# Four pairs instead of three by seven products in part two's down projection, with its left sides summed earlier

## The chip, the cores and the metric

The kernel runs on one core of a Trainium2 chip. The metric is the device time of one execution in microseconds (us); the number shown for a kernel is the median of several executions. Engines are named as in the profile: PE is TensorE's matmul, PEld its weight load, DVE VectorE, ACT ScalarE, POOL GpSimd, SP SyncE.

## The reference

One decoder layer on 256 tokens of width 2048, all in float32. Only its feed-forward halves matter here; there are two of them (before and after the token mixer), alike in shape:

```python
def swiglu(x, w_gu, w_down):
    gate, up = jnp.split(x @ w_gu, 2, axis=-1)
    return (jax.nn.silu(gate) * up) @ w_down

h = h + 0.5 * swiglu(rms_norm(h, ffn1_norm[i]), ffn1_w_gu[i], ffn1_w_down[i])
h = h + hybrid_mixer(...)
h = h + 0.5 * swiglu(rms_norm(h, ffn2_norm[i]), ffn2_w_gu[i], ffn2_w_down[i])
h = h + sigmoid(rms_norm(h, ple_norm[i]) @ ple_w_gate[i]) * (p[i] @ ple_w_proj[i])
```

`w_gu` is 2048 x 11264, `w_down` 5632 x 2048. Gate and up are each 11 blocks of 512 columns; the down projection sums over 5632 = 22 pairs of 256 rows.

## The kernel before

**Float32 by three matmuls.** Each matrix is split into a high part (rounded to the fp32r format) and a low part (the rest). A product is high x high + high x low + low x high: three matmuls of 128 x 128 by 128 x 512. For a weight, ACT makes the high part (`whi`, `shi`, a cast), DVE the low part (`wlo`, `slo`, a subtraction).

**Plain pairs.** A pair is 256 rows of a weight block of 512 columns, 512 KB. SP loads it into one of four buffers `raw`; ACT and DVE split it; PE does 2 row blocks x 2 token halves x 3 = 12 matmuls with it.

**Seven products.** Two weight blocks of 512 columns belong together, and a pair of rows over both of them is a 2 x 2 product of 2 x 2 blocks: 8 block products, 24 matmuls. For the first `ns` pairs of a group the kernel uses a scheme with seven products instead of eight (Winograd's form of Strassen's). Product i multiplies one right side (a quarter of the weights, or a sum of quarters) with one left side (a quarter of the activations, or a sum), and one call of `product` does it for all `ns` pairs: 3 x `ns` matmuls. The right sides come from four quarters that are loaded whole, each 128 x (512 `ns`) floats: B11 is `raw[0, 0]`, B12 `raw[0, 1]`, A12's partner `raw[1, 0]`, and `raw[1, 1]`. `all_sums` makes them one after the other: it casts and subtracts (`shi`, `slo`) and then adds the next quarter into `raw[0, 0]`. Such an addition is done by DVE (`add`, tile R) or by a DMA from POOL's queue which reads the quarter again from HBM and adds it in flight (`add_loaded`, line 314). `SEVEN` is the order of the seven.

**Left sides.** `halves` makes the sums of activations: per pair, DVE adds high and low part to S (128 x 512, line 456), does four additions on quarters of it (128 x 128, line 462), ACT casts it to `Sh`, DVE subtracts to `Sl`. `Sh` and `Sl` have one buffer each, which gate/up and down share in turn.

**Staging.** The 11 blocks are worked in three parts of 3, 4 and 4 (`PARTS`; part two is blocks 3 to 6). For each block in turn PE computes gate and up (a "gu" group), and DVE and ACT make `silu(gate) * up`, which is transposed through a scratch tensor in DRAM (`tb`, `scr2`, `tT`) and split into `hTh`, `hTl`. After the part's blocks come two "dn" groups, one for output columns 0 to 1023 (`nb` = 0) and one for 1024 to 2047, whose products are added to `h`. The seven products of a group are interleaved with the plain pairs of the group before it, one product after each plain pair: products of part two's first dn group lie among the plain pairs of the part's last gu group.

**What sets the order.** `plan` writes lists of plain pairs, products and loads; `order` says in which order weights are asked for. `lanes` are generators that are stepped once per plain pair, so that side work is spread out. Below that, a scheduler places the instructions on each engine; `tc.keep_in_program_order` pins an instruction. Each engine then runs its queue strictly in order.

**Buffers that matter.** `shi` and `slo` have two buffers each: the cast for product n + 2 waits until PE has finished product n. `raw` quarters (tile R) have four homes; a group's quarters are loaded into homes that the group before it has finished with.

**Part sizes before.** `NS_DOWN` is 2, 3 and 3 pairs by seven for the three parts; a gu group has `NS` = 4.

## Time and profile before

| | |
|---|---|
| time, median of 3 runs | 1944.34 us (1944.25 to 1946.11) |
| the profiled execution, its own time | 1945.28 us |
| its span, first to last instruction | 1943.6 us |
| PE busy | 1928.1 us, 99% of the span |
| DVE busy | 1570.4 us, 81% |
| ACT busy | 1164.1 us, 60% |
| DMA read and written | 475.05 MB, mean 244 GB/s |
| granted TensorE clock | 0.999 |

How to read it: times are microseconds from the start of the span. A matmul's row has a duration of some 0.39 us, but matmuls overlap; what counts is the distance from one start to the next. "idle before, releaser" is how long the engine stood still before the instruction and what ended that. Part two's down begins among gate and up of block 6, at 346 us in the first feed-forward and at 1489 us in the second; part three's at 593 and 1736 us.

### The profile page before, as it was taken

What the parts mean: (1) busy time and instruction counts of PE and PEld (TensorE: products, weight loads), DVE (VectorE), ACT (ScalarE), POOL (GpSimd) and SP (SyncE); (2) the same over time, 40 slices, a digit from 0 to 9 for tenths busy, and PEclk for the clock granted to TensorE, in tenths of its full rate; (3) what the DMA queues carried; (4) which work ended last, traced back from release to release, by engine and by line L of the source; (5) the groups of instructions that cost most, each with busy time, mean ns of one, the idle gap of its engine ahead of it and who ended that gap; (6) DMA issues with size and microseconds to landing.
All of it is one profiled execution on the core that took longest, in us unless ns stands there. A gap on an engine that the chain in (4) does not pass through costs nothing.

```text
span 1943.6 us, 24163 instructions
## 1 busy us (share of the span) xinstructions
PE 1928.1 (99%) x8884; PEld 1594.0 (82%) x8884; DVE 1570.4 (81%) x1703; ACT 1164.1 (60%) x1362; POOL 148.4 (8%) x226
## 2 busy tenths in 40 slices
PE   9999999999999999999999999999999999999998
PEld 7888888888888888878788888888888888888886
DVE  7879878997789766797856579899888987888865
ACT  6656666666666557664555456566556755657654
POOL 0010110000010000010100000010000100001000
PEclk9999999999999999999999999999999999999999
DMA  8778898888888765556565776788888987989764
GB/s 307 269 236 282 252 293 285 237 288 249 280 285 242 228 218 171 176 169 211 161 213 159 244 283 231 226 281 289 248 275 241 327 264 244 271 237 314 234 214 143
DMA packets 144182, 475.05 MB, mean 244 GB/s; under 512 B 19648, under 2 KB 47296, under 8 KB 129856
## 3 DMA queue, kind: packets, MB, share of 16 engines
q1 hardware_dynamic: 107200, 302.16, 44.4%
q0 software_dynamic: 25920, 160.44, 30.2%
q10 hardware_dynamic: 10944, 10.91, 1.8%
q8 instruction: 69, 1.13, 0.2%
q14 instruction: 49, 0.40, 0.1%
HBM read 451.44 MB, written 22.02 MB: 244 GB/s over the span
## 4 chain that ended last, share of the span: by engine, by line
PE 92%; DVE 5%; DMA 2%; issue 1%; ACT 0%; POOL 0%; SPq 0%; POOLq 0%; DVEq 0%; ACTq 0%
PE d L550 5%; PE d L552 5%; PE d L551 5%; PE u L551 5%; PE u L552 5%; PE u L550 5%; PE g L343 5%; PE g L342 5%; PE g L344 5%; PE g L551 4%; PE g L552 4%; PE pj L112 4%; PE pj L113 4%; PE pj L114 4%; PE g L550 4%; PE d L344 3%
## 5 line engine op out<-in xcount | busy, mean ns | idle before, releaser
L77 ACT CAST whi<-raw 128x1024 fp32r<-128x1024 f32 (+1 forms) x489 | 511.3, 1049 | 401.1 <-PE pj L114 106.6
L78 DVE TENSOR_TENSOR wlo<-raw,whi 128x1024 fp32r<-128x1024 f32 (+1 forms) x489 | 592.0, 1218 | 162.9 <-ACT whi L77 161.8
L299 DVE TENSOR_TENSOR slo<-R,shi 128x2048 fp32r<-128x2048 f32 (+2 forms) x224 | 444.9, 1989 | 132.1 <-ACT shi L298 130.1
L298 ACT CAST shi<-R 128x2048 fp32r<-128x2048 f32 (+2 forms) x224 | 373.9, 1671 | 141.5 <-DVE R L307 62.7
L112 PE MATMUL pj<-whi,nTh 128*128 128x512 f32 x448 | 179.4, 401 | 0.0
L113 PE MATMUL pj<-wlo,nTh 128*128 128x512 f32 x448 | 175.2, 391 | 1.1 <-DVE wlo L78 1.1
L114 PE MATMUL pj<-whi,nTl 128*128 128x512 f32 x448 | 174.9, 390 | 0.0
L550 PE MATMUL d<-whi,hTh 128*128 128x512 f32 x448 | 174.5, 390 | 0.0
L551 PE MATMUL d<-wlo,hTh 128*128 128x512 f32 x448 | 174.4, 389 | 0.0
L552 PE MATMUL d<-whi,hTl 128*128 128x512 f32 x448 | 173.4, 389 | 0.0
L551 PE MATMUL g<-wlo,nTh 128*128 128x512 f32 x400 | 156.6, 391 | 0.6 <-DVE wlo L78 0.6
L552 PE MATMUL g<-whi,nTl 128*128 128x512 f32 x400 | 156.0, 390 | 0.0
L551 PE MATMUL u<-wlo,nTh 128*128 128x512 f32 x400 | 155.8, 389 | 0.2 <-DVE wlo L78 0.2
L552 PE MATMUL u<-whi,nTl 128*128 128x512 f32 x400 | 155.6, 389 | 0.0
L550 PE MATMUL g<-whi,nTh 128*128 128x512 f32 x400 | 155.0, 391 | 0.6 <-ACT nTh L161 0.6
L550 PE MATMUL u<-whi,nTh 128*128 128x512 f32 x400 | 153.4, 389 | 0.0
L307 DVE TENSOR_TENSOR R<-R 128x2048 f32<-128x2048 f32 (+2 forms) x68 | 135.7, 1996 | 0.1
L113 PEld LDWEIGHTS pj<-wlo,nTh 128*128 128x128 f32 x448 | 84.2, 188 | 18.9 <-DVE wlo L78 2.7
L550 PEld LDWEIGHTS d<-whi,hTh 128*128 128x128 f32 x448 | 84.1, 188 | 18.1 <-ACT hTh L504 1.0
L552 PEld LDWEIGHTS d<-whi,hTl 128*128 128x128 f32 x448 | 84.1, 188 | 17.8
L114 PEld LDWEIGHTS pj<-whi,nTl 128*128 128x128 f32 x448 | 84.1, 188 | 17.6
L551 PEld LDWEIGHTS d<-wlo,hTh 128*128 128x128 f32 x448 | 84.1, 188 | 17.4
(332 smaller groups left out, 3447.0 us busy)
## 6 DMA issues: line engine op xcount, KB each, us to landing
raw<-in_w_gu SPq DMA_DIRECT2D x199, 512.0 KB, 5.8
raw<-in_w_down SPq DMA_DIRECT2D x112, 512.0 KB, 6.4
raw<-in_w_in SPq DMA_DIRECT2D x112, 512.0 KB, 3.4
R<-in_w_gu2q POOLq DMA_DIRECT2D x54, 1024.0 KB, 8.6
R<-in_w_gu1q POOLq DMA_DIRECT2D x48, 1024.0 KB, 8.3
raw<-in_w_out SPq DMA_DIRECT2D x32, 512.0 KB, 4.3
tT<-scr SPq DMA_DIRECT2D x22, 512.0 KB, 5.8
R<-in_w_down11q POOLq DMA_DIRECT2D x12, 768.0 KB, 7.0
```

The source lines that it names most:

```text
L77: nc.scalar.copy(hi[:, j, :], raw[:, j, :])
L78: nc.vector.tensor_tensor(out=lo[:, j, :], in0=raw[:, j, :], in1=hi[:, j, :], op=ALU.subtract)
L112: nc.tensor.matmul(outs[t], xh[:, c], whi[:, j, :], start=st, stop=False)
L113: nc.tensor.matmul(outs[t], xh[:, c], wlo[:, j, :], start=False, stop=False)
L114: nc.tensor.matmul(outs[t], xl[:, c], whi[:, j, :], start=False, stop=sp)
L298: keep(nc.scalar.copy(hi, w))
L299: nc.vector.tensor_tensor(out=lo, in0=w, in1=hi, op=ALU.subtract)
L307: keep(nc.vector.tensor_tensor(out=self.raw[x], in0=self.raw[x], in1=self.raw[y], op=ALU.add))
L344: nc.tensor.matmul(out, xl, whi[:, g, :], start=False, stop=sp, skip_group_check=True)
L550: nc.tensor.matmul(out, xh[:, c], whi[:, j, :], start=st, stop=False, skip_group_check=True)
L551: nc.tensor.matmul(out, xh[:, c], wlo[:, j, :], start=False, stop=False, skip_group_check=True)
L552: nc.tensor.matmul(out, xl[:, c], whi[:, j, :], start=False, stop=sp, skip_group_check=True)
```

## The change

- Part two's dn groups treat four pairs by seven products instead of three: quarters of 1 MB instead of 768 KB, products of 12 matmuls instead of 9, and four plain pairs per block of 512 columns instead of five.
- In the first dn group of parts two and three the order of the seven is `SEVEN_DOWN`: the product with A12, whose quarter `raw[1, 0]` needs no sum, comes second, and that quarter is loaded second.
- In the same groups B11 + B12 is no longer added by DVE but by a DMA from POOL's queue that reads B12 again.
- The first two left sides of these groups are summed one gu group earlier (`first_sides`), and only split where they were summed before; the others are summed straight from the transposed block `tT` rather than from `hTh` + `hTl`. Their additions on the way are no longer all where they were pinned.
- The part's last block is given one step less of distance in part two (`last`).

```diff
--- before.py
+++ after.py
@@ -28,10 +28,11 @@
 NS = 4
-NS_DOWN = tuple(3 if i1 - i0 == 4 else 2 for i0, i1 in PARTS)
+NS_DOWN = (2, 2), (4, 4), (3, 3)
...
 SEVEN = (0, 1, 2, 4, 3, 5, 6)
+SEVEN_DOWN = (0, 4, 1, 2, 3, 5, 6)
@@ -257,6 +258,7 @@
...
+            self.seven = SEVEN_DOWN if kind == "dn" and part and nb == 0 else SEVEN
@@ -283,7 +285,7 @@
...
-            use = (0, 0), (0, 1), (1, 1), (1, 0)
+            use = ((0, 0), (0, 1), (1, 1), (1, 0)) if self.seven is SEVEN else ((0, 0), (1, 0), (0, 1), (1, 1))
             self.home = dict(zip(use, free))
             return [("load", lambda q=q: self.load(*q)) for q in use]
@@ -313,10 +315,10 @@
...
-            for i in SEVEN:
+            for i in self.seven:
                 ws = halved(*((0, 0), (0, 0), (0, 0), (0, 1), (1, 0), (1, 1), (0, 0))[i])
                 if i == 0:
-                    add((0, 0), (0, 1))
+                    (add if self.seven is SEVEN else add_loaded)((0, 0), (0, 1))
                     add_loaded((0, 1), (1, 1))
                 elif i == 1:
                     add((0, 0), (1, 1))
@@ -371,8 +373,9 @@
...
             for nb in (0, 2):
-                src = [sources(f"w_down{n}{p}", nb + b) for b in range(2)]
-                groups.append(Group("dn", p, [x[0] for x in src], [x[1] for x in src], NS_DOWN[p], len(groups) % 2, nb))
+                src = [sources(f"w_down{n}{p}{nb // 2}", b) for b in range(2)]
+                groups.append(Group("dn", p, [x[0] for x in src], [x[1] for x in src], NS_DOWN[p][nb // 2],
+                                    len(groups) % 2, nb))
@@ -420,11 +423,8 @@
...
-    def halves(kind, his, los, ns, wait=0, at_once=2):
-
-
-        for _ in range(wait):
-            yield
+    def left_sides(kind, his, los):
+
         fp = current[0]
@@ -439,38 +439,64 @@
...
         sides[kind] = side
-
-        for g0 in range(0, ns, at_once):
-            n = min(at_once, ns - g0)
-            k0 = 2 * (g0 % 2)
-            hi, lo = (x[g0 // 2][:, k0:k0 + 2 * n] for x in (his, los))
-            keep = lambda ins: ins
-            if g0 == 2 and n == 1:
-
-                keep = tc.keep_in_program_order
-                yield
-            if n == 2:
-                x = fp.tile([P, 2 * NB], F32, tag="sil", name="S")
-            else:
-                x = act.tile([P, NB], F32, tag="nat", name="S", bufs=4)
-            keep(nc.vector.tensor_tensor(out=x, in0=hi.bitcast(F32).rearrange("p k x -> p (k x)"),
-                                         in1=lo.bitcast(F32).rearrange("p k x -> p (k x)"), op=ALU.add))
-            xv = x.rearrange("p (g j t y) -> p g j t y", g=n, j=2, t=2)
-            a11, a12, a21, a22 = (xv[:, :, j, t, :] for t in range(2) for j in range(2))
-            for o, y, z, op in ((a22, a21, a22, ALU.subtract), (a21, a11, a21, ALU.subtract),
-                                (a11, a22, a11, ALU.subtract), (a12, a11, a12, ALU.add)):
-                nc.vector.tensor_tensor(out=o, in0=y, in1=z, op=op)
-            sx = [y[:, g0:g0 + n].rearrange("p g j t y -> p (g j t y)") for y in (sh, sl)]
-            nc.scalar.copy(sx[0], x)
-            nc.vector.tensor_tensor(out=sx[1], in0=x, in1=sx[0], op=ALU.subtract)
-            if not g0 % 2 + n == 1 or g0 + n == ns:
-                yield
+        return sh, sl
+
+    def split_sums(s, g0, x, keep=lambda ins: ins):
+        n = x.shape[1] // NB
+        hi, lo = (y[:, g0:g0 + n].rearrange("p g j t y -> p (g j t y)") for y in s)
+        keep(nc.scalar.copy(hi, x))
+        keep(nc.vector.tensor_tensor(out=lo, in0=x, in1=hi, op=ALU.subtract))
+
+    def add_sides(x, src, keep=lambda ins: ins):
+
+        a11, a12, a21, a22 = x
+        b11, b12, b21, b22 = src
+        for o, y, z, op in ((a22, b21, b22, ALU.subtract), (a21, b11, b21, ALU.subtract),
+                            (a11, a22, b11, ALU.subtract), (a12, a11, b12, ALU.add)):
+            keep(nc.vector.tensor_tensor(out=o, in0=y, in1=z, op=op))
+
+    def sum_sides(x, his, los, g0):
+        n = x.shape[1] // NB
+        k0 = 2 * (g0 % 2)
+        hi, lo = (y[g0 // 2][:, k0:k0 + 2 * n].bitcast(F32).rearrange("p k x -> p (k x)") for y in (his, los))
+        nc.vector.tensor_tensor(out=x, in0=hi, in1=lo, op=ALU.add)
+        xv = x.rearrange("p (g j t y) -> p g j t y", g=n, j=2, t=2)
+        xs = [xv[:, :, j, t, :] for t in range(2) for j in range(2)]
+        add_sides(xs, xs)
+
+    def halves(kind, his, los, ns, wait=0):
+
+
+        for _ in range(wait):
+            yield
+        s = left_sides(kind, his, los)
+        for g0 in range(0, ns, 2):
+            x = current[0].tile([P, 2 * NB], F32, tag="sil", name="S")
+            sum_sides(x, his, los, g0)
+            split_sums(s, g0, x)
+            yield
...
     def ffn(n, nT, r, scale, next_norm, stat):
...
-            hTh, hTl = [], []
+            hTh, hTl, early, pending = [], [], [], []
+
+            def first_sides(p0):
+
+                for _ in range(4):
+                    yield
+                for g in range(2):
+                    x = act.tile([P, NB], F32, tag="nat", name="S", bufs=4)
+                    sum_sides(x, hTh[p0:], hTl[p0:], g)
+                    early.append(x)
+                    yield
+
+            def later_sides(s, made):
+
+                yield
+                for g, x in made:
+                    split_sums(s, g, x)
             def down_input(u, sil, th, tl, last):
@@ -503,6 +529,18 @@
                     tv = tT[:, :, t].rearrange("p q (j y) -> p q j y", j=4)
                     keep(nc.scalar.copy(hi, tv))
                     keep(nc.vector.tensor_tensor(out=lo, in0=tv, in1=hi, op=ALU.subtract))
+                if pending:
+                    s, ns = pending.pop()
+                    made = []
+                    for g in range(2, ns):
+                        x = act.tile([P, NB], F32, tag="nat", name="S", bufs=4)
+                        xv = x.rearrange("p (j t q y) -> p j t q y", j=2, t=2, q=4)
+                        k = 2 * (g - 2)
+                        add_sides([xv[:, j, t] for t in range(2) for j in range(2)],
+                                  [tT[:, :, t, 32 * (k + j):32 * (k + j) + 32] for t in range(2) for j in range(2)],
+                                  keep)
+                        made.append((g, x))
+                    lanes.add(1, later_sides(s, made))
             def gated(g):
                 sil = fp.tile([P, 2, NB], F32, tag="sil", name="sil")
@@ -523,8 +561,10 @@
                     lanes.add(1, halves("gu", *nT, NS))
                 elif dn and group.nb and group.follower:
                     lanes.add(1, halves("behind", *nxt, NS_BEHIND, 4))
+                elif not dn and group.part and group.follower.kind == "gu" and group.follower.follower.kind == "dn":
+                    lanes.add(1, first_sides(i0))
                 elif not dn and group.follower.kind == "dn" and not group.part:
-                    lanes.add(1, halves("dn", hTh[i0:], hTl[i0:], NS_DOWN[group.part]))
+                    lanes.add(1, halves("dn", hTh[i0:], hTl[i0:], NS_DOWN[group.part][0]))
                 if dn and group.last and nxt is None:
                     nxt = new_nT()
                 if group.banks is None:
@@ -532,11 +572,15 @@
                 for kind, one in todo:
...
-                        follower.product(SEVEN[one])
+                        follower.product(follower.seven[one])
                         if group.part and not dn and one == 5 and follower.kind == "gu" and \
                                 follower.follower.kind == "dn":
                             p = PARTS[group.part][0]
-                            lanes.add(1, halves("dn", Later(hTh, p), Later(hTl, p), NS_DOWN[group.part], 0, 1))
+                            lanes.finish(1)
+                            s = left_sides("dn", Later(hTh, p), Later(hTl, p))
+                            for g in range(2):
+                                split_sums(s, g, early.pop(0))
+                            pending.append((s, NS_DOWN[group.part][0]))
@@ -580,7 +624,7 @@
...
-                        last = (3 if i1 - i0 == 4 else 2) if len(hTh) == i1 else 0
+                        last = (6 - NS_DOWN[group.part][0] if i1 - i0 == 4 else 2) if len(hTh) == i1 else 0
                         gen = down_input(outs, sil, th, tl, last)
@@ -1362,7 +1406,8 @@
...
         for p, (i0, i1) in enumerate(PARTS):
-            _parted(m, f"w_down{n}{p}", b[:, 2 * i0:2 * i1], NS_DOWN[p])
+            for j in range(2):
+                _parted(m, f"w_down{n}{p}{j}", b[2 * j:2 * j + 2, 2 * i0:2 * i1], NS_DOWN[p][j])
```

The change moves instructions. Two places, both in the first feed-forward, where part two's last gate/up group (block 6) carries the products of part two's first down group.

On DVE, before: the stretch from the `slo` of that down group's first product (9 matmuls, 128x1536) to the `slo` of its third. R is a quarter of the weights, S the sum of a left side, the digits tell buffers apart.

```order
L299 TENSOR_TENSOR slo_2666<-R_2548,shi_2665 128x1536
L307 TENSOR_TENSOR R_2548<-R_2548,R_2584 128x1536
...
L78 TENSOR_TENSOR wlo_2711<-raw_2709,whi_2710 128x1024
L465 TENSOR_TENSOR Sl_2684<-S_2693,Sh_2683 128x512
L505 TENSOR_TENSOR hTl_2383<-tT_2604,hTh_2382 128x4x4x32 x2
L299 TENSOR_TENSOR slo_2728<-R_2548,shi_2727 128x1536
L487 STREAM_TRANSPOSE tb_2744<-sil_2526 128x4x128
L307 TENSOR_TENSOR R_2548<-R_2548,R_2625 128x1536
L487 STREAM_TRANSPOSE tb_2744<-sil_2526 128x4x128
L78 TENSOR_TENSOR wlo_2749<-raw_2747,whi_2748 128x1024
L456 TENSOR_TENSOR S_2770<-hTh_2382,hTl_2383 128x512
L299 TENSOR_TENSOR slo_2793<-R_2548,shi_2792 128x1536
```

The same place with the change, from the `slo` of the second product (A12's, from its own quarter R_2590) to that of the product after B11's second sum.

```order
L301 TENSOR_TENSOR slo_2738<-R_2590,shi_2737 128x2048
L456 TENSOR_TENSOR S_2714<-S_2714,tT_2610 128x128
L79 TENSOR_TENSOR wlo_2758<-raw_2756,whi_2757 128x1024
L513 STREAM_TRANSPOSE tb_2753<-sil_2526 128x4x128 x2
L448 TENSOR_TENSOR Sl_2678<-S_2709,Sh_2677 128x512
L448 TENSOR_TENSOR Sl_2678<-S_2714,Sh_2677 128x512
L301 TENSOR_TENSOR slo_2801<-R_2548,shi_2800 128x2048
L79 TENSOR_TENSOR wlo_2807<-raw_2805,whi_2806 128x1024
L309 TENSOR_TENSOR R_2548<-R_2548,R_2645 128x2048
L79 TENSOR_TENSOR wlo_2842<-raw_2840,whi_2841 128x1024
L301 TENSOR_TENSOR slo_2836<-R_2548,shi_2835 128x2048
L301 TENSOR_TENSOR slo_2875<-R_2637,shi_2874 128x2048
```

One DVE addition into R_2548 is gone (B11 + B12), the other stays between the third and the fourth product; the first sums of left sides are no longer here.

On POOL's queue, before: the loads of that group's quarters and the two additions by DMA, in the queue's order.

```order
L279 DMA R_2548<-in_w_down11q 128x1536
L279 DMA R_2584<-in_w_down11q 128x1536
L279 DMA R_2625<-in_w_down11q 128x1536
L279 DMA R_2633<-in_w_down11q 128x1536
L314 DMA R_2584<-in_w_down11q 128x1536
L314 DMA R_2548<-in_w_down11q 128x1536
L279 DMA R_2866<-in_w_down11q 128x1536
```

And with the change.

```order
L281 DMA R_2548<-in_w_down110q 128x2048
L281 DMA R_2590<-in_w_down110q 128x2048
L281 DMA R_2637<-in_w_down110q 128x2048
L316 DMA R_2637<-in_w_down110q 128x2048
L281 DMA R_2645<-in_w_down110q 128x2048
L316 DMA R_2548<-in_w_down110q 128x2048
L281 DMA R_2878<-in_w_down111q 128x2048
L316 DMA R_2548<-in_w_down110q 128x2048
```

There are three additions by DMA instead of two. The new one is the first into R_2548 (B11 + B12); the next group's first load (R_2878) now stands before the last addition into R_2548 and behind the new one.

## The prediction

> **What bounds the kernel.** First the page's busy times and the chain that ended last.

> ```profile
> PE 1928.1 (99%) x8884; PEld 1594.0 (82%) x8884; DVE 1570.4 (81%) x1703; ACT 1164.1 (60%) x1362; POOL 148.4 (8%) x226
> PE 92%; DVE 5%; DMA 2%; issue 1%; ACT 0%; POOL 0%; SPq 0%; POOLq 0%; DVEq 0%; ACTq 0%
> ```

> PE is busy 99% and makes up 92% of the chain. A busy PE may still run slowly, so next the busy times by stretch: 700 us of mostly feed-forward, and three stretches of part two's down in the first feed-forward (engine: us busy, x instructions; then clock, DMA share, GB/s).

> ```profile
> 1200.00:1900.00 700.00, 700.00 (x3088) 577.80 (x3087) 595.38 (x539) 428.93 (x438) 62.70 (x96) 1.00 0.84 264
> 346.00:365.00 19.00, 19.00 (x85) 15.49 (x84) 15.80 (x19) 10.31 (x13) 0.88 (x1) 1.00 0.73 185
> 365.00:377.00 12.00, 12.00 (x55) 9.93 (x54) 11.69 (x11) 9.10 (x10) 2.19 (x4) 1.00 0.99 371
> 377.00:413.00 36.00, 36.00 (x161) 29.80 (x160) 34.19 (x33) 24.19 (x24) 3.96 (x6) 1.00 0.97 319
> ```

> 700 / 3088 = 0.2267 us per matmul at full granted clock: the pace at which a matmul is worth something. In the short stretches the count holds matmuls cut by the edges, but PE stands nowhere. It is close to standing, though: DVE is busy 11.69 of 12 us and 34.19 of 36. The order of time shows how close (start, duration, engine).

> ```profile
> 352.21 1.19 DVE L78 TENSOR_TENSOR wlo<-raw,whi 128x1024 fp32r<-128x1024 f32 x1
> 352.52 0.62 PE L550 MATMUL g<-whi,nTh 128*128 128x512 f32 x2
> 353.45 0.50 PE L551 MATMUL g<-wlo,nTh 128*128 128x512 f32 x1
> ```

> The low part is written at 352.21 + 1.19 = 353.40, and the matmul that needs it starts at 353.45, out of its usual turn. So this place has no slack: whatever DVE is given here in addition, PE pays. That decides what the change is worth: matmuls saved, less what PE then waits for a late right side.

> **What is removed: matmuls.** With three pairs by seven a dn group of part two is 10 plain pairs x 12 + 7 x 9 = 183 matmuls, with four it is 8 x 12 + 7 x 12 = 180. Three fewer, in two groups, in two feed-forwards: 12 matmuls x 0.2267 = **2.72 us**. All of it lies on the path, since PE is the bound on both sides.

> **What DVE and ACT do for it.** The groups of instructions give the sizes (the number behind the comma is the mean, ns).

> ```profile
> L78 DVE TENSOR_TENSOR wlo<-raw,whi 128x1024 fp32r<-128x1024 f32 x487 | 590.6, 1220 | 160.2 <-ACT whi L77 159.1
> L299 DVE TENSOR_TENSOR slo<-R,shi 128x2048 fp32r<-128x2048 f32 x133 | 304.4, 2290 | 112.7 <-ACT shi L298 111.9 <-DMA raw<-in_w_gu 0.6
> L299 DVE TENSOR_TENSOR slo<-R,shi 128x1536 fp32r<-128x1536 f32 x56 | 97.9, 1754 | 10.3 <-ACT shi L298 10.1
> L307 DVE TENSOR_TENSOR R<-R 128x2048 f32<-128x2048 f32 x42 | 95.7, 2280 | 0.1
> L307 DVE TENSOR_TENSOR R<-R 128x1536 f32<-128x1536 f32 x16 | 27.9, 1746 | 0.0
> L298 ACT CAST shi<-R 128x1536 fp32r<-128x1536 f32 x8 | 11.9, 1483 | 5.5 <-PE d L344 2.1 <-PE g L344 1.7 <-PE u L344 1.7
> L298 ACT CAST shi<-R 128x2048 fp32r<-128x2048 f32 x1 | 1.9, 1913 | 0.0
> ```

> Per first dn group DVE gains 7 x (2.29 - 1.75) = 3.8 us for `slo` and 0.5 for the remaining addition, and loses two `wlo` (2.4) and the B11 + B12 addition (1.75): about zero. ACT gains 7 x 0.43 = 3.0 and loses two casts of some 1.05: it had 8.7 idle us in the first of the stretches. In sum neither costs anything; what matters is when each right side is ready. The order of PE is alternate there: product, plain pair, product, and so on, a set of 12 matmuls every 12 x 0.2267 = 2.72 us.

> **The moved left sides.** Two S additions (128x512) and eight quarter additions go from the stretch after 336 to before it: 2 x 0.6 + 8 x 0.2 = 2.8 us by the distances in the next fence. Before, DVE stands there for PE, so most of it goes into gaps (the number in brackets is the idle time before a row).

> ```profile
> 327.23 2.29 DVE L299 TENSOR_TENSOR slo<-R,shi 128x2048 fp32r<-128x2048 f32 x1 [1.99 <-ACT shi L298]
> 331.50 1.21 DVE L78 TENSOR_TENSOR wlo<-raw,whi 128x1024 fp32r<-128x1024 f32 x1
> 332.70 2.29 DVE L299 TENSOR_TENSOR slo<-R,shi 128x2048 fp32r<-128x2048 f32 x1
> 334.91 1.22 DVE L78 TENSOR_TENSOR wlo<-raw,whi 128x1024 fp32r<-128x1024 f32 x1
> 336.05 0.69 DVE L456 TENSOR_TENSOR S<-hTh,hTl 128x512 f32<-128x512 f32 x1
> 337.23 1.76 DVE L299 TENSOR_TENSOR slo<-R,shi 128x1536 fp32r<-128x1536 f32 x1 [0.50 <-ACT shi L298]
> 338.91 0.29 DVE L462 TENSOR_TENSOR S<-S 128x128 f32<-128x128 f32 x1
> 339.11 1.75 DVE L307 TENSOR_TENSOR R<-R 128x1536 f32<-128x1536 f32 x1
> 335.72 1.49 ACT L298 CAST shi<-R 128x1536 fp32r<-128x1536 f32 x1 [1.66 <-PE u L344]
> 346.62 0.39 PE L343 MATMUL d<-slo,hTh 128*128 128x512 f32 x1
> ```

> From start to start a large `slo` takes 2.21 us, a `wlo` 1.14, an S 0.60, a quarter addition 0.20. I walk the changed DVE queue from 327.23, where PE's release of a buffer pins it: `slo`, the two additions that remain in front of it, a `wlo` and the S work bring the last gate/up `slo` to 332.8 (332.70 before) and two `wlo` to 337.7. Then come two `Sl`. Their casts stand on ACT: `Sh` waits for PE's last use of the gate/up `Sh`, the product that also releases `shi` at 335.72; then the 1.9 us cast, `hTh` and the second `Sh` (0.5 each) end at 339.1. The first product's `slo` thus runs from 339.7 to 341.9, against 337.23 to 338.9 before. PE reads it at 346.62 in both kernels, as its list up to there is the same: slack 4.7 us instead of 7.7, no stall.

> **The new wait: B11 + B12 by DMA.** POOL's rows and the line of the additions by DMA over the whole run (issue to landing).

> ```profile
> 335.29 0.54 POOL L279 DMA_DIRECT2D R<-in_w_down11q  x1 [4.93 <-DVE slo L299]
> 341.16 0.89 POOL L314 DMA_DIRECT2D R<-in_w_down11q  x1 [5.33 <-DVE S L462]
> DMA to landing us min/median/max: 5.5/8.5/11.9
> ```

> The last load leaves POOL as before. The new addition may only start when `slo` has read B11, at 341.9, and lands 8.5 us later, 350.4. From there the chain is: cast 1.9 (352.3), `Sh` of the last sum, which stands behind that cast on ACT, 0.5 (352.8), `Sl` 0.6 (353.4), `slo` of the third product 2.2 (355.6; PE needs it at 346.62 + 4 x 2.72 = 357.5), `wlo` 1.1 (356.8), the DVE addition 2.2 (359.0), cast 1.9 (360.9), `slo` of the fourth product 2.3 (**363.2**). PE needs that at 346.62 + 6 x 2.72 = **362.9**: 0.3 us late. Behind the waiting cast on ACT stand the `Sh` counted here, a `whi` needed at 365.7 and the four stores of the transposed block; behind the addition on POOL only loads for the next group, 40 us ahead of use. A12's product second is what fills the time: with B11 + B12 in second place that `slo` would be due at 352.1, 3.5 us before it can be there. It needs ACT's copy of the first product out of PSUM, some 0.6 us after PE ends it, and starts 2.72 us after: free.

> Bounds: landing at 5.5 leaves 2.7 us over, at 11.9 PE waits 3.7 us. I take the median, 0.3 us in each feed-forward, **+0.6 us**.

> [...]

> **Part three** gets the new order and the new addition too, with its three pairs. Its product is 9 matmuls (2.04 us), the deadline 346.62 + 3 x 2.04 + 3 x 2.72, or 14.3 us behind the first product. The same walk with 1.75 for `slo`, 1.48 for the cast and one `Sh` less ends 17 us after the first `slo` (8.5 landing, then 1.5 + 1.7 + 1.1 + 1.7 + 1.5 + 1.75), which has some 5 us of slack at 341.4: 2 us over. Nothing. Nor does anything come back there, since PE's matmuls are as many.

> **Bytes.** Four plain pairs less (-2.1 MB), eight quarters larger by 256 KB (+2.1), additions by DMA 5 x 1.05 instead of 4 x 0.79 MB (+2.1), part three one more (+0.8): 2.9 MB more per feed-forward, beside 475 in all. Part two's one new addition lies at 342 to 350, where the DMA share is lowest (0.73 in the row from 346). Nothing, as long as loads keep their lead.

> **Sum.** 1945.28 (the profiled execution, span 1943.6 and 1.7 around it) - 2.72 + 0.6 = 1943.2; that execution lies 0.9 over the median, so by the median 1944.34 - 2.12 = **1942.2 us**.

> **Rivals.** (a) *The addition lands late.* For: the maximum of 11.9; DVE is without slack behind it. Against: the DMA engines are least busy just there. Each us beyond 8.2 costs 1 us per feed-forward; slower than before by over 0.2% (3.9 us) needs 3.3 us of stall in each, a landing of 11.5. At 11.9: 1944.34 - 2.72 + 2 x 3.7 = 1949.0. Chance 0.06. A milder form: POOL's issue is held up by one large `slo` of DVE, 2.3 us, so that PE waits 2.6 us in each: 1944.34 - 2.72 + 5.2 = 1946.8, no change; chance 0.05, counted in (c). [...] (b) *DMA becomes the bound* between 365 and 413, where its share is 0.97 to 0.99: 2.1 MB at 371 GB/s are 5.7 us per feed-forward if none hides, 1944.34 - 2.72 + 11.4 = 1953.0. Against: in that stretch plain loads shrink by as much as quarters grow, and part of the additions moves ahead of it. Chance 0.04. (c) *The stall eats the gain*, 1 to 3 us per feed-forward at landings of 9.5 to 11: 1943.6 to 1947.6, no change. Chance 0.25. (d) *No stall, and today's small ones vanish*: rows like 353.45 cost some 0.2 us in each of four down starts: 1941.6 - 0.8 = 1940.8. Chance 0.2; for more than 0.2% of gain it would take another 0.4 us, 0.05 of this. My forecast, 1941.6 to 1943.5, has 0.45.

> **How the numbers follow.** 0.2% of 1944.34 is 3.9 us, about what a measurement of this kernel tells from no change: under 1940.4 is faster, over 1948.2 slower. Faster 0.05, slower 0.10 from (a) and (b), the rest 0.85. The range goes down to (d), 1940.8, and up to 1946.0, under which most of (c) lies: some 0.2 is left outside.

> **What would show it.** Right: 12 matmuls fewer; the product after B11's second sum starts within 1 us of its turn; the B11 + B12 addition issues near 342 and lands near 350. Wrong: PE waiting for `slo` or `shi` of products three or four by more than 2 us; the first product's `slo` later than 343; a landing over 10; waits of `whi` for `raw` between 380 and 420; new waits in part three.

## The result, and the profile after

The changed kernel takes 1954.72 us (median of four executions, 1951.87 to 1956.21); the kernel before, beside it, 1944.3 (1944.12 to 1946.11). The ratio is 1.0051, with a 95% interval of 1.0037 to 1.0064: slower by about 10 us, where 1942.2 was predicted and the range ended at 1946.0. Run twice more it took 1953.4 us against 1945.0 and 1952.65 against 1944.59, ratios 1.0042 (1.0029 to 1.0054) and 1.004 (1.0028 to 1.0053). The profiled execution took 1951.87 us, the fastest of the four and 6.6 more than that of before.

The busy times and the chain of the changed kernel:

```profile
PE 1929.5 (99%) x8872; PEld 1593.6 (82%) x8872; DVE 1572.7 (81%) x1697; ACT 1169.7 (60%) x1356; POOL 152.9 (8%) x230
PE 87%; DVE 7%; issue 2%; DMA 2%; ACT 1%; ACTq 0%; POOL 0%; SPq 0%; DVEq 0%; POOLq 0%
```

The 12 matmuls are gone (x8884 before, x8872 now). Yet PE is busy 1.4 us longer instead of 2.7 us shorter, and DVE has a larger share of the chain. So two things are to be found: time in which PE stands, and time in which it runs slowly.

Where in the program: the starts of part two's down, part three's down and the next stage in the first feed-forward, before (first three rows) and after, from the order of time.

```profile
346.40 0.39 PE L342 MATMUL d<-shi,hTh 128*128 128x512 f32 x1
593.05 0.39 PE L342 MATMUL d<-shi,hTh 128*128 128x512 f32 x1
692.55 0.39 PE L112 MATMUL pj<-whi,nTh 128*128 128x512 f32 x1
```

```profile
345.74 0.39 PE L344 MATMUL d<-shi,hTh 128*128 128x512 f32 x1
597.04 0.39 PE L344 MATMUL d<-shi,hTh 128*128 128x512 f32 x1
696.76 0.39 PE L113 MATMUL pj<-whi,nTh 128*128 128x512 f32 x1
```

From the start of part two's down to that of part three's, 246.65 us became 251.30: +4.65, where -1.36 + 0.3 was predicted. From there to the mixer, 99.50 became 99.72: part three costs next to nothing. In the second feed-forward the same two distances grew by 3.64 and 0.04. All of the loss is made right where part two's down begins.

What PE waited for, over the whole run (the two groups that the kernel before does not have):

```profile
PE d L345 <- DVE slo L301: 5.7, 2, 2.9
...
PE d L344 <- ACT shi L300: 0.4, 1, 0.4
```

Two waits, of 2.9 and 2.8 us, one in each feed-forward, on the low part of a right side. The order of time on PE shows which, and what comes behind it:

```profile
357.15 0.50 PE L344 MATMUL d<-shi,Sh 128*128 128x512 f32 x1 [0.37 <-ACT shi L300]
360.60 0.50 PE L345 MATMUL d<-slo,Sh 128*128 128x512 f32 x1 [2.94 <-DVE slo L301]
...
361.32 0.63 PE L344 MATMUL d<-shi,Sh 128*128 128x512 f32 x1
361.75 0.63 PE L345 MATMUL d<-slo,Sh 128*128 128x512 f32 x1
...
364.31 0.43 PE L345 MATMUL d<-slo,Sh 128*128 128x512 f32 x1
```

It is the third product, the one that needs B11 + B12. Its first matmul goes at 357.15, the next only at 360.60. Then, from 361.32 on, matmuls start 0.43 us apart instead of 0.227, until 364.31. The busy times by stretch say why (engine columns as in the prediction; the clock is the third number from the end). First the changed kernel, then the kernel before at the same place.

```profile
356.00:361.00 5.00, 1.69 (x7) 0.87 (x6) 3.35 (x3) 2.56 (x3) 0.00 (x0) 1.00 0.67 254
361.00:364.40 3.40, 3.40 (x10) 2.63 (x9) 3.40 (x3) 0.41 (x1) 0.00 (x0) 0.50 0.43 154
...
1507.80:1511.20 3.40, 3.40 (x9) 2.63 (x8) 3.40 (x3) 0.77 (x1) 0.00 (x0) 0.50 0.45 154
```

```profile
361.00:364.40 3.40, 3.40 (x17) 2.81 (x16) 1.67 (x2) 3.07 (x5) 0.00 (x0) 1.00 0.99 298
```

Behind each of the two waits the granted clock is 0.50 for 3.4 us: PE is "busy" for all of it, with 9 or 10 matmuls in place of 16 or 17. That is 1.7 us of PE's time each, which no view of waits shows. As a count of where the time went, the sum for the profiled execution closes: -2.72 (matmuls) + 5.7 + 0.4 (waits) + 2 x 1.7 (half clock) = +6.8, against +6.6 measured. It closes better in total than in its parts: PE's idle time grew by 5.2 us (15.5 to 20.7) where the new waits make 6.1, since small waits of the kernel before are gone, and its busy time by 1.4 where matmuls and half clock make 0.7. Whether the half clock is also a cause, so that the time without it would be 3.4 us shorter, is a question of its own (runs 5, 6, 7 and 11).

Why the right side is late: ACT and DVE in the order of time.

```profile
355.19 1.91 ACT L300 CAST shi<-R 128x2048 fp32r<-128x2048 f32 x1 [5.64 <-DMA R<-in_w_down110q]
357.01 0.61 ACT L447 CAST Sh<-S 128x512 fp32r<-128x512 f32 x1
```

```profile
357.65 0.69 DVE L448 TENSOR_TENSOR Sl<-S,Sh 128x512 fp32r<-128x512 f32 x1 [6.01 <-ACT Sh L447]
358.26 2.29 DVE L301 TENSOR_TENSOR slo<-R,shi 128x2048 fp32r<-128x2048 f32 x1
```

The chain is the one that the prediction walked: landing, cast 1.9, `Sh`, `Sl`, `slo`, 5.4 us from 355.19 to 360.55 (5.2 predicted). Only its start is late: 355.2 instead of 350.4. POOL's queue shows what stands ahead of that addition, and the lines of the additions (336 to 343, then 1480 to 1492) and of the load behind 335 say how long each took from issue to landing:

```profile
335.04 0.89 POOL L316 DMA_DIRECT2D R<-in_w_down110q  x1 [5.33 <-DMA R<-in_w_down110q]
335.69 0.78 POOL L281 DMA_DIRECT2D R<-in_w_down110q  x1
341.78 0.87 POOL L316 DMA_DIRECT2D R<-in_w_down110q  x1 [5.31 <-issue]
```

```profile
DMA to landing us min/median/max: 9.8/11.6/13.3
...
DMA to landing us min/median/max: 9.3/10.8/12.2
...
DMA to landing us min/median/max: 13.1/13.1/13.1
```

The addition of B22 to B12 (1 MB) goes at 335.04 and lands 9.8 us later, at 344.8; the last load (1 MB) goes behind it at 335.69 and lands at 348.8; the new addition goes at 341.78, exactly where predicted (341.9), with 7 us of that load still to come, and lands 13.3 us later, at 355.1. The three transfers of one queue land at distances of 4.0 and 6.3 us, though they were issued 0.65 and 6.09 us apart. In the second feed-forward the new one takes 12.2 us. The DMA engines are also fuller there than in the kernel before (share: the second number from the end; first the kernel before, then the changed one):

```profile
342.00:350.00 8.00, 8.00 (x37) 6.62 (x36) 8.00 (x15) 5.44 (x8) 0.05 (x1) 1.00 0.79 165
```

```profile
342.00:350.00 8.00, 8.00 (x37) 6.63 (x36) 8.00 (x15) 3.58 (x5) 1.21 (x2) 1.00 0.99 311
```

So there are two explanations for the late landing, the place in the queue and full engines; run 2 tells them apart.

### The profile page after: what moved, and what is told of

The parts are those of the page before. It is cut to its first block, busy times and chain, and to the rows that moved or that the text cites. A ratio compares the mean times of both kernels' runs of the same rounds, so it can differ in the third digit from the quotient of the medians.

```text
span 1950.2 us, 24115 instructions
## 1 busy us (share of the span) xinstructions
PE 1929.5 (99%) x8872; PEld 1593.6 (82%) x8872; DVE 1572.7 (81%) x1697; ACT 1169.7 (60%) x1356; POOL 152.9 (8%) x230
## 2 busy tenths in 40 slices
DMA packets 143605, 480.81 MB, mean 247 GB/s; under 512 B 19584, under 2 KB 47232, under 8 KB 125952
## 4 chain that ended last, share of the span: by engine, by line
PE 87%; DVE 7%; issue 2%; DMA 2%; ACT 1%; ACTq 0%; POOL 0%; SPq 0%; DVEq 0%; POOLq 0%
PE d L594 4%; PE d L595 4%; PE d L596 4%; PE g L345 4%; PE g L346 4%; PE g L344 4%; PE u L594 4%; PE u L595 4%; PE u L596 4%; PE pj L113 4%; PE pj L114 4%; PE pj L115 4%; PE g L595 4%; PE g L596 4%; PE g L594 4%; PE d L345 3%
## 5 line engine op out<-in xcount | busy, mean ns | idle before, releaser
L78 ACT CAST whi<-raw 128x1024 fp32r<-128x1024 f32 (+1 forms) x481 | 503.5, 1050 | 380.2 <-PE pj L115 108.0
L79 DVE TENSOR_TENSOR wlo<-raw,whi 128x1024 fp32r<-128x1024 f32 (+1 forms) x481 | 582.9, 1218 | 155.1 <-ACT whi L78 152.3
L301 DVE TENSOR_TENSOR slo<-R,shi 128x2048 fp32r<-128x2048 f32 (+2 forms) x224 | 460.0, 2056 | 130.1 <-ACT shi L300 128.3
L300 ACT CAST shi<-R 128x2048 fp32r<-128x2048 f32 (+2 forms) x224 | 386.1, 1725 | 176.9 <-DVE R L309 82.8
L594 PE MATMUL d<-whi,hTh 128*128 128x512 f32 x416 | 162.2, 390 | 0.0
L595 PE MATMUL d<-wlo,hTh 128*128 128x512 f32 x416 | 161.9, 389 | 0.0
L596 PE MATMUL d<-whi,hTl 128*128 128x512 f32 x416 | 161.2, 390 | 0.0
L113 PEld LDWEIGHTS pj<-whi,nTh 128*128 128x128 f32 x448 | 84.2, 188 | 16.7
L594 PEld LDWEIGHTS d<-whi,hTh 128*128 128x128 f32 x416 | 78.1, 188 | 17.2 <-ACT hTh L530 1.3
L596 PEld LDWEIGHTS d<-whi,hTl 128*128 128x128 f32 x416 | 78.1, 188 | 17.1 <-DVE hTl L531 0.5
```

Source lines behind the costliest of these rows:

```text
L78: nc.scalar.copy(hi[:, j, :], raw[:, j, :])
L79: nc.vector.tensor_tensor(out=lo[:, j, :], in0=raw[:, j, :], in1=hi[:, j, :], op=ALU.subtract)
L113: nc.tensor.matmul(outs[t], xh[:, c], whi[:, j, :], start=st, stop=False)
L300: keep(nc.scalar.copy(hi, w))
L301: nc.vector.tensor_tensor(out=lo, in0=w, in1=hi, op=ALU.subtract)
L594: nc.tensor.matmul(out, xh[:, c], whi[:, j, :], start=st, stop=False, skip_group_check=True)
```

## The experiments

In all of these, "before" is the kernel before, run on the same chip beside them: 1944.64 us (33 runs) for the first four, 1944.8 (6 runs) for number 7, 1944.59 (9 runs) for 10 and 11, 1945.0 (15 runs) for the others.

**1. B11 + B12 by DVE again.**

```diff
-                    (add if self.seven is SEVEN else add_loaded)((0, 0), (0, 1))
+                    add((0, 0), (0, 1))
```

> The changed kernel, but B11 + B12 of the first down group in parts two and three is added by DVE again instead of by DMA. Theory (the new addition by DMA lands late because it stands third behind two other 1 MB transfers of POOL's queue): no wait for a DMA is left at the third product, PE idles under 0.5 us there and no stretch of half clock follows; DVE has 2.2 us more to do, so that the fourth product's slo is about 1 us late: 1942.5 to 1945 us. Rival (the third product is late by DVE's own load or by the moved left sides): the idle time at the third or fourth product stays at 3 us or more, with half clock behind it, 1950 us or more.

Measured: 1943.8 us, ratio 0.9995 (0.9986 to 1.0004), 10.9 us under the changed kernel's median. PE's waits in part two's down:

```profile
PE d L345 <- DVE slo L301: 0.5, 2, 0.2
PE d L344 <- ACT part L352: 0.4, 2, 0.2
```

The clock stays at 1.00 through the place. So the whole loss hangs on this one line; the four pairs, the moved left sides and the new order of the products are not its cause. And the work that the DMA was to take from DVE fits there.

**2. The same DMA, ahead of the other addition on POOL's queue.** The new addition stays; the addition of B22 to B12 is pinned behind it.

```diff
-                nc.gpsimd.dma_start(out=self.raw[x], in_=self.quarters[y[1]][y[0]], accum_op=ALU.add)
+                dma = nc.gpsimd.dma_start(out=self.raw[x], in_=self.quarters[y[1]][y[0]], accum_op=ALU.add)
+                if self.seven is not SEVEN and x == (0, 1):
+                    tc.keep_in_program_order(dma)
```

> The changed kernel, with the one DMA that adds the fourth quarter into B12's tile pinned behind the new addition B11 + B12 in POOL's queue; nothing else moves. Theory (place in the queue): the new addition has one transfer ahead of it instead of two and lands 8 to 10 us after its issue instead of 12 to 13; PE's idle time at the third product falls from 3.3 us to under 1 us, the half clock is gone in both feed-forwards: 1941.5 to 1944 us. Rival (such an addition takes 12 us there wherever it stands, because the DMA engines are shared with SP's loads): landing stays at 12 to 13 us and the time at 1951 to 1956.

Measured: 1944.9 us, ratio 1.0001 (0.9992 to 1.001). POOL's rows, then the landing times of the last load by itself and of the new addition by itself, and the stretch in which it is on its way:

```profile
336.51 0.54 POOL L281 DMA_DIRECT2D R<-in_w_down110q  x1 [5.99 <-ACT Sh L449]
342.60 1.79 POOL L316 DMA_DIRECT2D R<-in_w_down110q  x2 [5.54 <-issue]
```

```profile
DMA to landing us min/median/max: 5.0/5.0/5.0
...
DMA to landing us min/median/max: 8.1/8.1/8.1
```

```profile
342.00:350.00 8.00, 8.00 (x37) 6.60 (x36) 8.00 (x16) 4.43 (x5) 2.16 (x3) 1.00 0.95 222
```

The load ahead has nothing in front of it now and lands in 5.0 us, at 341.5, before the addition leaves; the addition lands in 8.1 us instead of 13.3. Same instruction, same bytes, same time of issue within 0.8 us, engines as busy (0.95 against 0.99, though they move 222 GB/s against 311): the place in the queue makes the 5 us. The addition that was pinned behind shows it from the other side. It goes at 343.2, in the same stretch, with one transfer ahead of it, and takes 14.4 us, the largest of the two additions' times:

```profile
DMA to landing us min/median/max: 8.1/11.3/14.4
```

It lands 6.8 us behind the one ahead; in the changed kernel the new addition landed 6.3 us behind the load ahead. The wait of 2.9 us and the half clock are gone, and 9.8 us of the changed kernel's median come back. This is the prediction's own picture, landing near 350 and all, and it still gains nothing that can be measured; the median is 0.9 us above what this run was expected to take at most. A wait on the low part of an activation appears, whose cause was not looked into, beside small ones on `slo`; the span is 0.7 us shorter than before, of the 2.72 saved.

```profile
PE d L598 <- DVE hTl L533: 1.5, 2, 0.9
...
PE d L347 <- DVE slo L301: 0.5, 3, 0.2
```

**3. Four pairs only in part two's second group**, with the rest of the change, the DMA too, but on quarters for three pairs (768 KB) in the first group.

```diff
-NS_DOWN = (2, 2), (4, 4), (3, 3)
+NS_DOWN = (2, 2), (3, 4), (3, 3)
...
-                            pending.append((s, NS_DOWN[group.part][0]))
+                            pending.append((s, NS_DOWN[group.part][1]))
```

> The changed kernel with three pairs by seven in part two's first down group and four in its second one only (quarters of 768 KB in the first; left sides for four pairs are still made). Theory: the first group's additions are 0.75 MB, land by 10 us, and PE does not stall; 6 matmuls fewer than before are worth 1.36 us: 1942.5 to 1944 us. Rival (the new order and the moved left sides cost time by themselves): 1946 or more, with PE waiting in both down starts.

Measured: 1943.78 us, ratio 0.9994 (0.9985 to 1.0003); the waits of `d` on `slo` are 0.4 us in all. With smaller quarters the same DMA comes in time: part two's five additions in the first feed-forward land 7.1 to 10.2 us after their issue.

**4. Three pairs everywhere**, so the change without its saving.

```diff
-NS_DOWN = (2, 2), (4, 4), (3, 3)
+NS_DOWN = (2, 2), (3, 3), (3, 3)
```

> The changed kernel with three pairs by seven in both down groups of part two, as before: new order, B11 + B12 by DMA and the moved left sides alone. Theory: no matmul is saved and no stall of over 1 us appears: 1943.5 to 1945.5 us. Rival (these parts cost by themselves): 1947 or more, the loss of the change without its gain.

Measured: 1944.7 us, ratio 1.0001 (0.9992 to 1.001). Moving the left sides, the order of the products and the DMA cost nothing by themselves that can be measured.

**5. and 6. Is the half clock made by the wait?** Runs 1 to 4 took wait and half clock away together. These two make waits in another place, in the kernel before: in the mixer's output matmul, DVE repeats the subtraction of four weight pairs (the same value is written again).

```diff
+        for _ in range(again):
+            nc.vector.tensor_tensor(out=lo, in0=raw, in1=hi, op=ALU.subtract)
...
+    again = {len(order) + x: n for x, n in ((3, 4), (10, 5), (17, 6), (25, 7))}
```

The second run has 4 repeats at each of the four.

> The kernel before the change, with one addition to its work in the mixer's output matmul (1064 to 1151 us), where the trace of before shows DVE at 53.84 of 87 us and every low half ready 3.2 us before PE uses it: the subtraction wlo <- raw, whi of the pairs with number 3, 10, 17 and 25 is repeated 4, 5, 6 and 7 times (the same value is written again). One repeat is about 1.14 us from start to start, so PE should stand for m x 1.14 - 3.2 = 1.4, 2.5, 3.6 and 4.8 us, 12.3 us in all. Both theories agree on these waits. Theory A (a long enough stand of PE by itself costs a further stretch at half clock, as behind the two stands of 2.95 us in the changed kernel): granted clock 0.5 for about 3.4 us behind the waits of 3.6 and 4.8 us, perhaps behind that of 2.5, none behind 1.4; each such stretch adds about 1.7 us, so 1944.6 + 12.3 + 3.4 to 5.1 = 1960.3 to 1962.0. Rival B (the half clock in the changed kernel belongs to something else there, such as what the DMA or ACT does at that place): full clock behind all four, 1944.6 + 12.3 = 1956.9.

> As the dose run, but each of the four pairs is repeated 4 times: four waits of PE of about 1.4 us, 5.4 us in all. Both theories: no stretch at half clock, 1944.6 + 5.4 = 1950.0. If the half clock came with any stand of PE, or with added work on DVE, it would show here too: 4 x 1.7 = 6.8 us more, 1956.8.

Measured: 1979.76 us (ratio 1.0179, 1.0165 to 1.0192) and 1970.64 us (1.0132, 1.0118 to 1.0145). Both expectations missed the size: PE's waits were 3.5, 5.6, 7.9 and 9.1 us in the first, 3.5, 4.3, 4.4 and 4.4 in the second, since the repeats do not stay behind one pair but mix with its neighbours' subtractions and use up their lead as well. So the second run was no control with short waits. What both show is the half clock, behind all eight waits. The second of the four waits of the second run, and the stretch behind it:

```profile
1096.00:1101.80 5.80, 1.50 (x7) 0.89 (x5) 5.58 (x5) 1.05 (x1) 0.00 (x0) 0.86 0.62 182
1101.80:1107.10 5.30, 5.27 (x13) 4.13 (x13) 0.00 (x0) 0.59 (x1) 0.00 (x0) 0.50 0.62 207
```

No product, no DMA addition and no new work on ACT is there. In these two runs a wait of PE by itself brought the half clock; rival B falls. Taken at 0.50, as in the second row, the mean clock of stretches of 10 us makes the time at half clock behind the four waits 3.4, 6.8, 10.2 and 10.2 us in the first run and 3.4, 6.8, 3.4 and 6.8 in the second: one, two or three times the 3.413 us that the record of the granted clock has for each of the changed kernel's two.

**7. Shorter waits.** The doses are 3, 2, 3 and 2.

```diff
-    again = {len(order) + x: n for x, n in ((3, 4), (10, 5), (17, 6), (25, 7))}
+    again = {len(order) + x: n for x, n in ((3, 3), (10, 2), (17, 3), (25, 2))}
```

> The dose run again with smaller doses, since 4 repeats already made PE stand for 3.5 to 4.4 us: the subtraction of the pairs 3, 10, 17 and 25 is repeated 3, 2, 3 and 2 times. From the 3.5 and 4.4 us of 4 repeats and 1.14 us a repeat: waits of PE of about 2.4, 2.1, 3.3 and 2.1 us, 9.9 in all. Theory A1 (the clock is halved once PE stands for most of one 3.41 us interval of a fixed grid): half clock behind the wait of 3.3, none behind those of about 2.1, and 2.4 undecided; 1945.0 + 9.9 + 1.7 = 1956.6, or 1958.3 with the 2.4. Theory A2 (any wait over about 1.5 us does it): four stretches, 1945.0 + 9.9 + 6.8 = 1961.7.

Measured: 1958.21 us, ratio 1.0068 (1.005 to 1.0086). The first three waits, each from the waits of its own stretch:

```profile
PE wo L116 <- DVE wlo L80: 1.2, 1, 1.2
...
PE wo L116 <- DVE wlo L80: 0.6, 1, 0.6
...
PE wo L116 <- DVE wlo L80: 2.1, 1, 2.1
```

The stretch behind the first wait, and the third wait with the stretch behind it:

```profile
1073.80:1083.00 9.20, 9.18 (x40) 7.59 (x41) 4.85 (x5) 3.14 (x4) 0.00 (x0) 1.00 0.87 270
1113.00:1115.50 2.50, 0.35 (x2) 0.00 (x0) 2.50 (x4) 0.97 (x1) 0.00 (x0) 1.00 0.08 15
1115.90:1119.30 3.40, 3.40 (x10) 2.65 (x9) 1.90 (x3) 0.00 (x0) 0.00 (x0) 0.51 0.94 302
```

Full clock behind 1.2 us (and behind 0.6, not shown), half clock behind 2.1. (The fourth dose fell on the start of the next stage, a wait of 4.5 us, and had half clock, 0.50, for 6.7 us.) The waits came out other than expected again, so the total says nothing, and by these three waits alone A2 would fit. The granted clock's records bear out A1's grid, with a lower line than A1 had taken. In the record of before the one change lies 1931.944 us behind the first entry, which is 566 x 3.4133; in that of the changed kernel the five changes lie 104, 105, 440, 441 and 568 times 3.4133 us behind it, each within 0.002 us. Counted by these intervals, at full clock PE stood for at most 1.16 us in any that had full clock behind it, in both records, and for 2.94 and 2.61 us in the changed kernel's two that had half clock behind them (the ends of the programs, where it stood throughout, had it too). One interval from either side, with a wait of 1.83 us in run 11 and with the larger part of a wait of 3.0 us in run 10:

```profile
366.20:369.61 3.41, 1.66 (x7) 1.40 (x8) 2.83 (x2) 3.41 (x4) 0.90 (x1) 1.00 0.76 279
...
358.52:361.94 3.42, 1.42 (x6) 1.20 (x7) 3.42 (x3) 0.00 (x0) 0.00 (x0) 1.00 0.36 126
```

PE stands for 1.75 and 2.00 us of the two. Behind the first the clock stays full, behind the second it is 0.50. So A2, any wait over about 1.5 us, falls with the 1.83 us of run 11; the 2.1 us here lay within one interval. (PE's standing time rests on ends of matmuls that the profile models.) In this run, where nothing else is late behind the waits, the half clock is paid in full: waits 1.2 + 0.6 + 2.1 + 4.5 = 8.4, three times 3.4 us at half clock 3 x 1.7 = 5.1, together 13.5; measured 13.4.

**8. A version that might beat both**: four pairs in part two's second group alone, as in run 3, and three instead of two in part one's second group.

```diff
-NS_DOWN = (2, 2), (4, 4), (3, 3)
+NS_DOWN = (2, 3), (3, 4), (3, 3)
...
+            for _ in range(99 if g0 and ns == 3 else 0):
+                yield
...
-                    lanes.add(1, halves("dn", hTh[i0:], hTl[i0:], NS_DOWN[group.part][0]))
+                    lanes.add(1, halves("dn", hTh[i0:], hTl[i0:], NS_DOWN[group.part][1]))
...
+                if dn and not group.part and not group.nb:
+                    lanes.finish(1)
...
-                            pending.append((s, NS_DOWN[group.part][0]))
+                            pending.append((s, NS_DOWN[group.part][1]))
```

The third left side of part one is summed on its own, held back until the work on the part's first down group begins.

> A version that may beat both: the changed kernel with four pairs by seven only in the second dn group of part two (as in the run with 3 and 4), and three instead of two pairs by seven in the second dn group of part one. By the matmuls 6 fewer in part two and 6 fewer in part one, 12 x 0.2267 = 2.7 us less than before: 1944.6 - 2.7 = 1941.9. The run with 3 and 4 alone showed 0.86 of its 1.36 us. If the third sum of the left side and the larger right sides cost DVE as much as the matmuls save in part one: 1943.5 to 1944.5.

Measured: 1945.96 us, ratio 1.0007 (0.9998 to 1.0016). The matmuls are 12 fewer than before, but the waits take the gain back:

```profile
PE d L344 <- ACT shi L300: 1.9, 2, 1.0
```

This row is in part one, once in each feed-forward (none in run 3); another 0.8 us are on a `slo`. It is the bad case of the expectation and a little worse, and the wait is on ACT's cast, where the expectation had named DVE.

**9. and 10. The changed kernel again**, unaltered.

> The changed kernel unaltered, on the same chip as the three above. If the two stands of PE and the two stretches at half clock are a fixed property of the program, 1951 to 1956 as before, with both stretches in the profile; if the stretch at half clock depends on when the stand falls (its length was only just enough), some executions lack one or both and lie 1.7 or 3.4 us lower.

> The changed kernel unaltered, on the same chip as the run with the 12 further matmuls, to compare them: 1953 to 1955.

Measured: 1953.4 us (1951.29 to 1954.22) and 1952.65 (1952.23 to 1953.01), the second a little under its expectation. In the profile of the first the landing is later still (13.8 us) and `d` waits 6.2 us for `slo`; both stretches of half clock are there, and so they are in the second's. With a mean clock of 0.996 or 0.997 in every execution of the changed kernel, the stall is a fixed property of the program. That its length was "only just enough" for the half clock was the author's estimate: in the changed kernel's first trace PE stood for 2.94 and 2.61 us of the two intervals ahead of the half clock, and in run 10 2.00 us in one had half clock behind them too.

**11. Keep PE busy during the wait.** Runs 5 to 7 leave open whether, in the changed kernel, the half clock is paid on top of the wait. Here the third product begins with 12 matmuls that only need its `shi`; the product then starts its PSUM bank anew and overwrites what they left.

```diff
+            if i == 1 and self.ns == 4 and self.seven is SEVEN_DOWN:
+                xh = sides[self.kind](i, 0)[0]
+                for _ in range(12):
+                    nc.tensor.matmul(out, xh, whi[:, 0, :], start=True, stop=True, skip_group_check=True)
             for g in range(self.ns):
```

> The changed kernel, with 12 further matmuls (12 x 0.2267 = 2.7 us of PE) in front of the third product of part two's first dn group, into its own PSUM bank, which the product then starts anew; they need only its shi, which is there 3 us before its slo. So PE works through most of the time in which it stood, and waits for at most some 0.5 us there. All theories: full clock behind it. Theory X (the half clock is paid on top of the wait, 1.7 us each): 3.4 us less than the changed kernel. Theory Y (the fourth product's low part is late by the same chain: in the changed kernel it is ready at 368.22 and read at 368.47, so PE at full clock would have come 1.7 us too early for it): the same time as the changed kernel, within 0.7 us, with a new wait of some 1.5 us on slo in the fourth product, near 366 and near 1513.

Measured: 1955.0 us (1953.12 to 1957.43), ratio 1.0056 (1.0042 to 1.0069), beside the changed kernel's 1952.65: no gain, so theory X falls. Its median lies 2.35 us above, more than the 0.7 us that theory Y allowed, though the intervals overlap; theory Y can be read only from the profiled execution, the fastest of the five. It has a span of 1951.1 us, the changed kernel's beside it 1951.2. What PE waits for in it, and the order of time at the third and the fourth product:

```profile
PE d L349 <- DVE slo L301: 3.8, 4, 1.8
```

```profile
356.82 3.02 PE L344 MATMUL d<-shi,Sh 128*128 128x512 f32 x12 [0.24 <-ACT shi L300]
360.26 0.50 PE L349 MATMUL d<-slo,Sh 128*128 128x512 f32 x1 [0.20 <-DVE slo L301]
...
365.63 0.49 PE L348 MATMUL d<-shi,Sh 128*128 128x512 f32 x1
367.95 0.50 PE L349 MATMUL d<-slo,Sh 128*128 128x512 f32 x1 [1.83 <-DVE slo L301]
```

The 12 matmuls fill the wait, the clock stays full (mean 0.999 in place of 0.997), and PE comes to the fourth product 1.7 us earlier, only to wait 1.83 us for its `slo` (1.6 in the second feed-forward). There theory Y is right: the end is set by the chain on DVE, ACT and the DMA, and that chain kept its pace with PE at full clock and at half. From the end of the third product's `slo` to the end of the fourth's it takes 7.69 us here and 7.67 in the changed kernel. In the changed kernel the same product shows it as an exact fit, `slo` written until 365.93 + 2.29 = 368.22 and read at 368.47:

```profile
365.93 2.29 DVE L301 TENSOR_TENSOR slo<-R,shi 128x2048 fp32r<-128x2048 f32 x1 [0.91 <-ACT shi L300]
```

```profile
368.47 0.39 PE L345 MATMUL d<-slo,Sh 128*128 128x512 f32 x1
```

So the half clock here takes the place of a wait and costs at most the 0.25 us between these two times. (The other executions of this run are 1 to 4 us longer at mean clocks of 0.997 and 0.998. They were not profiled, and why they are longer stays open.)

## Why the prediction was wrong, point by point

**Matmuls saved.** Right: 12 fewer. 2.72 us is what they are worth at PE's pace; in runs 1 and 3, which have no stall, 0.8 and 0.9 us of the 2.72 and 1.36 were left in the medians. Their intervals hold nothing, and also all of the 1.36 and, at the very edge, all of the 2.72. Run 2's ends at 1.6 us less than before: there "All of it lies on the path" did not hold.

**DVE and ACT, and the moved left sides.** Right. The first product's `slo` ran from 338.96 to 341.24, where 339.7 to 341.9 was worked out, and PE, which came for it at 345.97 and not at 346.62, did not wait. Runs 1 and 4 bear it out: neither the DVE addition nor the moved sums cost anything that shows. By run 1 the sentence that PE pays for whatever DVE is given there was too strong: DVE had the addition of 2.28 us back, and `d` waited 0.9 us in all.

**The new wait: B11 + B12 by DMA.** This is the step that failed. The prediction took the landing at the median of all additions in the kernel before, 8.5 us, argued with low DMA use between 342 and 350, and said "The last load leaves POOL as before". It did leave at about the same time (335.69 instead of 335.29), but POOL's list in front of the prediction had the fact that was missing: with the change an addition of 1 MB stands right before that last load, and the new one right behind it. When the new one was issued, the load still had 7 us to go. So the landing was 13.3 us in the first feed-forward and 12.2 in the second. The median describes additions that have the queue nearly to themselves: by the issues and landings in the trace of before, 49 of its 60 additions left with no other transfer of POOL on its way, 11 with one, none with two. It also mixes sizes: the 34 additions of 1 MB alone have a median of 8.9. Run 2 gave this one a place with none ahead and measured 8.1. The argument from the low DMA share was no help either: 0.73 was the share of the kernel before, and the change's own transfers filled the place.

With the measured landing the prediction's own arithmetic gives the result. It had each us beyond a landing of 8.2 cost one us, counted up to the fourth product: 5.1 and 4.0, so 1945.28 - 2.72 + 9.1 = 1951.7 for the profiled execution, which took 1951.87. For the profiles of runs 9 and 10 (landings of 13.8 and 12.4, then 12.6 and 13.4) the same sum gives 1952.4 and 1952.2; they took 1953.81 and 1952.9. So the agreement to 0.2 us is partly luck, and what the slower executions, up to 1956.21, have beyond that is not explained. The other terms held: issue at 341.78 instead of 341.9, chain 5.4 instead of 5.2 us.

**The fourth product**, to be late by 0.3 us, is late by all of that, and hides it: in the changed kernel it appears as 3.3 us of wait at the third product and 1.7 us of half clock behind it, 5.0 together, and as no wait of its own; in run 11 as 0.4 us (0.24 + 0.20) and 2.7 us of additional matmuls at the third and 1.83 at the fourth, 5.0 again.

**The half clock** is in no part of the prediction, and the trace of before, whose longest wait of PE is 1.2 us, shows it only at its end, where PE has nothing left to do. First read, it looked like the part of the loss that had been missed, 3.4 us. Run 11 says that it is not: without it the span of the profiled execution is the same.

**The rival that came true** is (a), the addition lands late, with a chance of 0.06. Its path from a late landing to PE's wait, its rule and its threshold (a landing of 11.5 for a kernel slower by 0.2%) were right; what made the landing late, the transfers ahead in the queue, it did not name. Its chance rested on 11.9 as the worst case, because that was the maximum of the trace; but a maximum is a bound only for the situations that the trace holds, and it holds no addition behind two transfers in flight.

**Its milder form**, POOL held by DVE, did not occur: the addition's issue took 0.87 us, as before. No run shows the hold of 2.3 us from which its 1946.8 is added up: issuing took 0.86 to 0.91 us for all 64 additions of the changed kernel and 0.87 to 0.91 for the 60 of before, and in run 2 0.89 and 1.22 for the two at this place. **(b) The DMA engines as the bound**: did not occur; PE has no wait on `whi` behind 380. **(d) Small stalls vanish** (its 1941.6 is 1944.34 - 2.72): could not come true with the stall; in run 2, without it, other small waits came instead.

**Part three, bytes.** Right: +0.2 and +0.04 us, and no new waits there. (The walk for part three adds up to 17.75 us, not 17, so 1.5 us were over and not 2.) The DMA moved 480.81 MB, 5.8 more than before, as worked out.

**What would show it.** The signs named were the right ones: a landing over 10 and a wait of more than 2 us in the third product were both there.

## What to carry to other kernels

Price a DMA by its place in its queue, not by a median over the run: list what is issued ahead on the same queue and not yet landed, and count from there. In part two's first down group, with four pairs, an addition of 1 MB landed 6.2 to 6.8 us behind the transfer ahead of it that was still on its way (the changed kernel and run 2), against 8.1 us from its issue with none ahead (run 2). A half clock behind a wait of PE was a loss of its own here only where nothing was late behind it: in the mixer it added 1.7 us for each 3.4 us at half clock (run 7), in part two's down at most 0.25 us, because the next operand came from the same late chain; a count of where the time went that closes is not yet a cause. And where PE is the bound with DVE at 95%, a few matmuls less may be worth less than they count: of 2.7 us saved, no gain clear of the noise was left in any version without the stall, and in two of them (runs 2 and 8) new waits stand beside the saving.
